# Late squares in one layer only, block weights with priority, and copies ahead of cuts in a two-layer decoder trunk

## The chip, the cores and the metric

The kernel runs on one core of a Trainium2 chip. The metric is device time in microseconds (us) of one execution. TensorE (PE in the profile) multiplies matrices and loads weights (PEld), VectorE (DVE) and ScalarE (ACT) work on tiles, GpSimd (POOL) does small odds and ends, SyncE (SP) starts the DMAs.

## The reference

Two layers work on 512 tokens of width 1024, in float32. Layer 0 mixes by sliding-window attention and a short gated convolution, layer 1 by chunked gated linear attention. Behind its mixer each layer has a gated MLP with a convolution over tokens and then a gate on a per-layer embedding:

```python
x = x + _conv_ffn(_rms_norm(x, ffn_norm[i]), ffn_w_up[i], ffn_conv_w[i], ffn_conv_b[i], ffn_w_down[i])
x = x + _per_layer_embedding(x, p[i], ple_norm[i], ple_w_gate[i], ple_w_proj[i])

def _per_layer_embedding(x, p_i, norm, w_gate, w_proj):
    gate = jax.nn.sigmoid(_rms_norm(x, norm) @ w_gate)
    return gate * (p_i @ w_proj)
```

The RMS norm needs, for each token, the sum of squares over the 1024 features. The kernel multiplies by the unnormed operand and scales the result by the norm afterwards, so the sums are needed later than the operand.

## The kernel before

**Data.** The stream `x` is kept as eight tiles `xT[m]` of 128 features by 512 tokens. A float32 product is made of three matmuls: each operand is split into a rounded high part (ACT copies it, `wh` for weights) and the rest (DVE subtracts, `wl`). `cut` and `cut_blocks` do this for weights, `split` for activations. Weights arrive by DMA in a `raw` buffer, two of which take turns; `wh` and `wl` have three buffers each.

**Seven products.** Where a block product allows it, `seven` computes a 2 x 2 block product with seven block multiplications in place of eight. It needs sums and differences of blocks on both sides. For weights these are made by `first_forms` (L864, L865) and `more_forms` (L872, L875) on DVE and cut at L840 (ACT) and L841 (DVE): `plain`, `t13`, the narrow `t2`, and `last`. For activations they are made by `blocks`: row m is scaled by the norm's gain (L302), and for each pair of rows the forms `e1`, `s12`, `o`, `s34` are built (L316 to L322 on DVE) and split (L109 on ACT, L110 on DVE). `seven` is a generator. Between its products ACT copies partial results from one PSUM bank to another (L897), because several results share a part; the product that follows in that bank waits for the copy.

**Squares.** `squares(m)` squares row m on ACT (L289 for row 0, L293 for the others) and adds it to `acc` on DVE (L294). `by_token` then transposes `acc` on PE (L345), and the sums and the inverse root are made from it. In `blocks`, the squares of both rows of a pair are traced behind the pair's forms and tied by `behind` to the last split, on ACT and on DVE; their scratch tile comes from `spare()`. Without `spare()`, `squares` takes its scratch from a tag "sq" with two buffers, which the narrow cut `t2` uses as well.

**Stages.** In each layer `ffn` runs the up-projection in groups, then `down`, whose last steps call `finish`, that is `blocks`, for each row. Then layer 0 runs `ple0` and layer 1 runs `ple1`. `ple0` has four stages g = 0 to 3. Each runs one `seven` for two output tiles, with the projection of the embedding in between, and `close` applies the gate of the stage before: DVE at L1408 to L1411, a sigmoid on ACT (L1414), DVE at L1415 and L1416, and then the squares for layer 1's first norm. `prepare` makes the weights of the next stage. In stage 0 the sums of squares are transposed between the third and the fourth step of `seven`. In stage 3 `enter` splits the rows for layer 1. `ple1` runs its products in an order written out by hand: the first product, two steps of the second, the transposes of `acc` at L345, and then the rest.

**Order.** Inside `manual_schedule(engines={ET.PE})` PE follows the written order; in `ple1`, ACT and DVE do as well. All other order on ACT and DVE is made by a planner when the program is built: of the instructions that are ready by its own costs, it takes the one traced first. `high_priority(offset=n)` moves instructions n places forward in that order. `issue_after(ins)` queues what is traced in it, on the engine of `ins`, behind `ins`, without a wait for its end. On the chip each engine takes its instructions in the planned order.

Of the kernel before, what the change touches and what calls it, by code (L numbers as in the profile page):

```python
# [63 lines left out]
class Kernel:  # L64
# [231 lines left out]
    def blocks(self, m, gain, scratch, tags, spare):  # L296


        nc = self.nc
        H = S // 2  # L300
        gx = scratch()
        nc.scalar.activation(gx, self.xT[m], AF.Copy, scale=gain[:, m : m + 1])  # L302

        def parts(x):
            w = x.shape[1]
            h, l = self.pair(self.fp, *tags)
            self.last_split = self.split((h[:, :w], l[:, :w]), x)
            return [(h[:, c], l[:, c]) for c in HALVES]

        if m % 2 == 0:  # L310
            self.even = gx
            self.e1 = parts(gx[:, :H])
        else:
            e, o = self.even, gx
            s12, s34 = scratch(), scratch()
            nc.vector.tensor_tensor(s12[:, :H], e[:, H:], o[:, H:], ALU.add)  # L316
            nc.vector.tensor_tensor(s12[:, H:], s12[:, :H], e[:, :H], ALU.subtract)
            s12p = parts(s12)
            op = parts(o)
            self.odd_split = self.last_split  # L320
            nc.vector.tensor_tensor(s34[:, :H], e[:, :H], e[:, H:], ALU.subtract)
            nc.vector.tensor_tensor(s34[:, H:], o[:, :H], s12[:, H:], ALU.subtract)  # L322
            s34p = parts(s34)
            self.forms.append(
                dict(e1=self.e1[0], o1=op[0], o2=op[1], s1=s12p[0], s2=s12p[1], s3=s34p[0], s4=s34p[1])
            )
            with self.behind(self.last_split):
                self.squares(m - 1, spare())
                self.squares(m, spare())

    @contextmanager
    def behind(self, pair):
# [552 lines left out]
    def seven(self, od, ws, x, keep=None, swift=False, pair=None):  # L885


        nc = self.nc
        H = S // 2
        mm = nc.tensor.matmul  # L890
        W, V = self.pa(), self.pa()[:, :H]
        X, Y = self.ps(), self.ps()
        plain, t13, t2 = ws

        def copy(out, src):
            with self.tc.high_priority(offset=60) if swift else nullcontext():
                return nc.scalar.copy(out, src)  # L897

        def product(out, w, c, x, first=False):
            kw = dict(skip_group_check=True)  # L900
            for j in range(ND // 2):
                (wh, wl), (xh, xl) = w(j, c), x(j)
                mm(out, wh, xh, start=first and j == 0, stop=False, **kw)  # L903
                mm(out, wh, xl, start=False, stop=False, **kw)  # L904
                mm(out, wl, xh, start=False, stop=j == ND // 2 - 1, **kw)  # L905

        left, right = HALVES
        product(W[:, left], plain, 0, x["e1"], True)
        copy(X[:, left], W[:, left])
        copy(Y[:, left], W[:, left])  # L910
        yield
        product(V, t13, 0, x["s1"], True)
        more = V
        if keep is not None:
            more = keep()
            copy(more, V)
        product(X[:, left], plain, 1, x["o1"])
        product(Y[:, left], t2, 0, x["s2"])
        yield copy(X[:, right], Y[:, left])
        with self.behind(pair):  # L920
            last = self.cut_blocks(od)
        product(X[:, right], t13, 1, x["s3"])
        yield copy(Y[:, right], X[:, right])
        product(Y[:, left], last, 1, x["s4"])
        product(X[:, right], last, 0, x["o2"])
        yield X, Y, more

    def ffn(self, i, project, next_gain):


        nc, a, tc = self.nc, self.a, self.tc
# [4 lines left out]
        mine, other = (("a0", "a1"), ("b0", "b1"))[:: 1 - 2 * i]  # L936
        with tc.tile_pool(name=f"ffn{i}", bufs=1) as fp:
# [4 lines left out]
            def both():  # L942
                return fp.tile([P, 2, S], F32, tag="zt", name=self.nm("zt"), bufs=2)
# [132 lines left out]
            steps, w0c, w1c = ready  # L1076
            with tc.manual_schedule(engines={ET.PE}):
                late = begin(0, steps, w0c)
                close = lambda: None
                for d in range(groups):  # L1080
                    g, y = both(), both()
                    copied = next(steps)
# [6 lines left out]
                    copied = next(steps)  # L1089
# [6 lines left out]
                    if d + 1 < groups:  # L1096
                        steps, w0c, w1c = prepare(d + 1, copied)
# [29 lines left out]
            def spare():  # L1127
                return fp.tile([P, S], F32, tag="z", name=self.nm("sq"), bufs=3)

            finish = lambda m: self.blocks(m, next_gain, half, mine if m < 4 else other, spare)  # L1130
            work = [lambda f=f: split_blocks(f) for f in (14, 16, 18, 20)]
            for f in (8, 10, 12):
                split_pair(f)
# [231 lines left out]
    def ple0(self, fp, both, next_gain):  # L1365


        nc, a, tc = self.nc, self.a, self.tc
        H = S // 2
        forms = self.forms  # L1370
        wg = a["ple_w_gate"][0].rearrange("(k p) n -> p k n", p=P)
        operands = {q: (lambda j, q=q: forms[j][q]) for q in ("e1", "o1", "o2", "s1", "s2", "s3", "s4")}
        groups = ND // 2

        def load(g):
            raw = self.raw(ND, 2 * P)
            nc.sync.dma_start(raw, wg[:, :, 2 * P * g : 2 * P * (g + 1)])
            return raw

        def result():  # L1380
            return fp.tile([P, S], F32, tag="z", name=self.nm("so"), bufs=3)

        def prepare(raw, odd=None, last=None):
            ev, od = self.by_parity(raw)
            return self.seven(od, self.seven_forms(ev, od, raw, odd), operands, lambda: result()[:, :H], True, last)

        pT = self.pT
        steps = prepare(load(0), self.odd_split, self.last_split)
        wj = self.wj

        def proj(m):
            pj = self.pa()
            c = slice(m * P, (m + 1) * P)
            for k in range(2):
                self.mm3(pj, [w[:, k, c] for w in wj], pT[k], start=k == 0, stop=k == 1)
            return pj

        def enter(*ms):
            for m in ms:
                hl = self.pair(self.fp, "b0", "b1")  # L1400
                self.split(hl, self.xT[m], next_gain[:, m : m + 1])
                self.xg.append(hl)

        def close(g, sums, pjs):
            X, Y, more = sums
            gates = both()
            h2 = lambda x: x.rearrange("p (u t) -> p u t", u=2)
            nc.vector.tensor_tensor(gates[:, 0], X, R, ALU.mult)  # L1408
            s = gates[:, 1]
            nc.vector.tensor_tensor(h2(s), h2(Y), more.unsqueeze(1).to_broadcast([P, 2, H]), ALU.add)  # L1410
            nc.vector.tensor_tensor(s, s, R, ALU.mult)  # L1411
            for c in range(2):
                m, s = 2 * g + c, gates[:, c]
                nc.scalar.activation(s, s, AF.Sigmoid)  # L1414
                nc.vector.tensor_tensor(s, s, pjs[c], ALU.mult)  # L1415
                nc.vector.tensor_tensor(self.xT[m], self.xT[m], s, ALU.add)  # L1416
                self.squares(m)

        late = None
        with tc.manual_schedule(engines={ET.PE}):  # L1420
            pjs = [proj(0), proj(1)]
            for g in range(groups):
                ends = g + 1 == groups
                if not ends:
                    raw = load(g + 1)
                next(steps)
                if late:
                    close(*late)
                if ends:
                    enter(0, 1)  # L1430
                next(steps)
                if ends:
                    enter(2, 3)
                if g:
                    pjs = [proj(2 * g)]
                else:
                    self.end_norm()
                    self.begin_norm(None)
                next(steps)
                if g:  # L1440
                    pjs.append(proj(2 * g + 1))
                last = steps
                if not ends:
                    steps = prepare(raw)
                late = g, next(last), pjs
                if g == 0:
                    R = self.spread()
            enter(4, 5)
            close(*late)
            enter(6, 7)  # L1450
        self.end_norm()
# [651 lines left out]
```

## Time and profile before

| | us |
|---|---|
| median of 3 runs | 1204.91 (1203.3 to 1205.11) |
| the profiled execution | 1205.17 |
| its span, first to last instruction | 1203.3 |
| PE busy in the span | 1190.9 |
| DVE busy | 993.7 |
| ACT busy | 690.4 |

The span is what the profile's views divide; 1.87 us of the execution lie around it. A row of the order in time has the start, the duration, the engine, the line, the operation, the tiles (out<-in), the shape and the count of instructions merged; a bracket at its end has the idle time of the engine before it and what ended it. Durations overlap a little, since the engines are pipelined. `ple0` runs from about 521 to 577 us, `ple1` from 1139 us to the end.

### The profile page before, as it was taken

To read this page: it belongs to the slowest core of one execution; us is meant where nothing else is said; L and a number is where in the kernel's file an instruction comes from. 1 tells how busy PE (TensorE), PEld (TensorE's weight loads), DVE (VectorE), ACT (ScalarE), POOL (GpSimd) and SP (SyncE) were. 2 spreads that over 40 slices of the span, in tenths; PEclk is the share of its full clock that TensorE was granted. 3 is DMA by queue.
4 is the path that set the end of the run, shared out by engine and by line. 5 is a ranking of instruction groups with operands and counts; after the bars stand their busy time and mean duration, and the time that the engine had idled before them with its cause. 6 is when DMAs were issued, how large, how long until landed. Compare 5 with 4: busy or idle time off the path is not lost.

```text
span 1203.3 us, 20222 instructions
## 1 busy us (share of the span) xinstructions
PE 1190.9 (99%) x8218; PEld 1081.1 (90%) x8218; DVE 993.7 (83%) x1593; ACT 690.4 (57%) x1137; POOL 45.5 (4%) x64
## 2 busy tenths in 40 slices
PE   9999999999999999999999999999999999999988
PEld 8877789999999989889878988899999999888877
DVE  6787687898999986899779876778989999978575
ACT  7466565656565653756563654555556556646364
POOL 2610000000000000000100000000000000000000
PEclk9999999999999999999999999999999999999999
DMA  7232222333332442321322212223242423323501
GB/s 222 72 99 78 74 88 71 107 105 106 106 106 89 147 133 89 105 71 61 120 87 70 89 53 75 84 93 118 72 141 71 130 81 115 125 86 123 184 1 70
DMA packets 112928, 117.76 MB, mean 98 GB/s; under 512 B 2840, under 2 KB 107858, under 8 KB 112836
## 3 DMA queue, kind: packets, MB, share of 16 engines
q1 hardware_dynamic: 112000, 115.88, 29.8%
q8 instruction: 64, 1.05, 0.4%
q0 software_dynamic: 560, 0.42, 0.3%
q14 instruction: 28, 0.23, 0.1%
q10 hardware_dynamic: 276, 0.18, 0.1%
HBM read 114.37 MB, written 2.10 MB: 97 GB/s over the span
## 4 chain that ended last, share of the span: by engine, by line
PE 89%; DVE 6%; ACT 3%; DMA 1%; issue 1%; POOL 0%; ACTq 0%; DVEq 0%
PE ps L171 11%; PE ps L172 11%; PE ps L173 11%; PE pa L173 7%; PE pa L172 7%; PE pa L171 7%; PE ps L903 6%; PE ps L905 6%; PE ps L904 6%; PE pa L905 2%; PE pa L903 2%; PE pa L904 2%; PE ps L1499 1%; PE ps L1501 1%; PE ps L1500 1%; DVE wl L152 1%
## 5 line engine op out<-in xcount | busy, mean ns | idle before, releaser
L152 DVE TENSOR_TENSOR wl<-raw,wh 128x1024 fp32r<-128x1024 f32 (+4 forms) x142 | 162.5, 1146 | 41.1 <-ACT wh L151 40.5
L151 ACT ACTIVATE wh<-raw 128x1024 fp32r<-128x1024 f32 (+4 forms) x142 | 141.2, 997 | 86.9 <-PE ps L172 54.4
L840 ACT ACTIVATE wh<-raw 128x1024 fp32r<-128x1024 f32 x90 | 95.4, 1062 | 128.3 <-DVE raw L865 86.2
L958 DVE SCALAR_TENSOR_TENSOR zt<-z,vfa,zt 128x510 f32<-128x510 f32 (+1 forms) x176 | 130.7, 743 | 0.3
L841 DVE TENSOR_TENSOR wl<-raw,wh 128x1024 fp32r<-128x1024 f32 x90 | 109.9, 1221 | 14.8 <-ACT wh L840 14.6
L173 PE MATMUL pa<-b,wl 128*128 128x256 f32 x352 | 97.3, 276 | 0.0
L173 PE MATMUL pa<-a,wl 128*128 128x256 f32 x352 | 97.3, 276 | 0.0
L172 PE MATMUL pa<-a,wh 128*128 128x256 f32 x352 | 97.2, 276 | 0.0
L171 PE MATMUL pa<-a,wh 128*128 128x256 f32 x352 | 97.2, 276 | 0.0
L171 PE MATMUL pa<-b,wh 128*128 128x256 f32 x352 | 97.2, 276 | 0.0
L172 PE MATMUL pa<-b,wh 128*128 128x256 f32 x352 | 97.2, 276 | 0.0
L956 ACT ACTIVATE zt<-z,vfb 128x512 f32<-128x512 f32 x88 | 71.3, 810 | 17.9 <-DVE z L948 8.8
L171 PE MATMUL ps<-b,wh 128*128 128x512 f32 x192 | 76.7, 399 | 0.1
L172 PE MATMUL ps<-b,wh 128*128 128x512 f32 x192 | 75.1, 391 | 0.0
L173 PE MATMUL ps<-b,wl 128*128 128x512 f32 x192 | 75.0, 391 | 0.0
L173 PEld LDWEIGHTS pa<-b,wl 128*128 128x128 f32 x352 | 66.1, 188 | 0.1
L172 PEld LDWEIGHTS pa<-a,wh 128*128 128x128 f32 x352 | 66.1, 188 | 0.0
L172 PEld LDWEIGHTS pa<-b,wh 128*128 128x128 f32 x352 | 66.1, 188 | 0.0
L171 PEld LDWEIGHTS pa<-a,wh 128*128 128x128 f32 x352 | 66.1, 188 | 0.0
L171 PEld LDWEIGHTS pa<-b,wh 128*128 128x128 f32 x352 | 66.1, 188 | 0.0
L173 PEld LDWEIGHTS pa<-a,wl 128*128 128x128 f32 x352 | 66.1, 188 | 0.0
L903 PE MATMUL ps<-four,wh 128*128 128x256 f32 x232 | 64.7, 279 | 0.0
(468 smaller groups left out, 3761.5 us busy)
## 6 DMA issues: line engine op xcount, KB each, us to landing
raw<-in_ffn_w_up_dram SPq DMA_DIRECT2D x42, 1024.0 KB, 5.0
raw<-in_ffn_w_down_dram SPq DMA_DIRECT2D x13, 1024.0 KB, 5.2
raw<-in_hy_w_in_dram SPq DMA_DIRECT2D x8, 1024.0 KB, 5.1
raw<-in_gla_w_in_dram SPq DMA_DIRECT2D x8, 1024.0 KB, 5.1
raw<-in_ffn_w_down_dram SPq DMA_DIRECT2D x8, 768.0 KB, 5.3
raw<-in_ple_w_gate_dram SPq DMA_DIRECT2D x6, 1024.0 KB, 5.5
raw<-in_hy_w_out_dram SPq DMA_DIRECT2D x16, 256.0 KB, 4.1
raw<-in_gla_w_out_dram SPq DMA_DIRECT2D x4, 1024.0 KB, 5.1
```

What stands on the lines that cost most here:

```text
L151: nc.scalar.activation(hv, v, AF.Copy)
L152: self.rest_cut = nc.vector.tensor_tensor(lv, v, hv.bitcast(F32), ALU.subtract)
L171: mm(out, lh, rh, start=start, stop=False, **kw)
L172: mm(out, lh, rl, start=False, stop=False, **kw)
L173: mm(out, ll, rh, start=False, stop=stop, **kw)
L840: nc.scalar.activation(h, src, AF.Copy)
L841: nc.vector.tensor_tensor(l, src, h.bitcast(F32), ALU.subtract)
L903: mm(out, wh, xh, start=first and j == 0, stop=False, **kw)
L904: mm(out, wh, xl, start=False, stop=False, **kw)
L905: mm(out, wl, xh, start=False, stop=j == ND // 2 - 1, **kw)
L956: nc.scalar.activation(y, z, AF.Identity, scale=w2[:, f : f + 1], bias=bb[:, f : f + 1])
L958: nc.vector.scalar_tensor_tensor(out=y[:, tap:], in0=z[:, : S - tap], scalar=w[:, f : f + 1], in1=y[:, tap:], op0=ALU.mult, op1=ALU.add,)
```

## The change

Three things are changed.

1. `blocks` in layer 1 is given no `spare`. There each row's squares are traced right after the row's own forms, with scratch from the tag "sq", and are tied to nothing. In layer 0 the squares stay as they were.
2. In `seven`, if `swift` is set (only `ple0` sets it), the cut of the last block weights (`last`: one ACT copy and one DVE subtraction) is moved 60 places forward in the planner's order.
3. In stage 0 of `ple0`, the weights of stage 1 are prepared under `issue_after(copied.ins)`: their ACT cuts are queued behind the copy from Y to X that the second step of `seven` gives back.

```diff
             self.forms.append(
                 dict(e1=self.e1[0], o1=op[0], o2=op[1], s1=s12p[0], s2=s12p[1], s3=s34p[0], s4=s34p[1])
             )
-            with self.behind(self.last_split):
-                self.squares(m - 1, spare())
-                self.squares(m, spare())
+            if spare:
+                with self.behind(self.last_split):
+                    self.squares(m - 1, spare())
+                    self.squares(m, spare())
+        if not spare:
+            self.squares(m)
...
         yield copy(X[:, right], Y[:, left])
-        with self.behind(pair):
+        with self.behind(pair), self.tc.high_priority(offset=60) if swift else nullcontext():
             last = self.cut_blocks(od)
...
-            finish = lambda m: self.blocks(m, next_gain, half, mine if m < 4 else other, spare)
+            finish = lambda m: self.blocks(m, next_gain, half, mine if m < 4 else other, None if i else spare)
...
-                next(steps)
+                copied = next(steps)
                 if ends:
                     enter(2, 3)
...
                 if not ends:
-                    steps = prepare(raw)
+                    with nullcontext() if g else tc.issue_after(copied.ins):
+                        steps = prepare(raw)
```

## The prediction

> **What bounds the kernel now.** I read the page first, then the stretches of the span, then the order in time of the three busy engines where the matmul engine stands still.
>
> ```profile
> span 1203.3 us, 20222 instructions
> PE 1190.9 (99%) x8218; PEld 1081.1 (90%) x8218; DVE 993.7 (83%) x1593; ACT 690.4 (57%) x1137; POOL 45.5 (4%) x64
> ```
>
> TensorE (PE) is busy 1190.9 of 1203.3 us, and the change adds or removes no matmul. So it can move the time only through the 12.4 us in which PE is idle, and through the speed at which PE runs. The view of stretches shows where these are: columns are the length, then busy time (and instructions) of PE, weight loads, DVE, ACT and POOL, then the granted clock, the DMA share and GB/s.
>
> ```profile
> 524.00:540.00 16.00, 14.40 (x112) 13.06 (x111) 14.81 (x25) 10.59 (x21) 1.43 (x1) 1.00 0.21 67
> 540.00:570.00 30.00, 30.00 (x232) 28.05 (x230) 28.22 (x41) 20.78 (x37) 0.00 (x0) 1.00 0.20 61
> 570.00:600.00 30.00, 28.98 (x172) 26.64 (x173) 21.23 (x32) 17.21 (x31) 3.87 (x7) 1.00 0.36 115
> 1139.00:1155.00 16.00, 12.59 (x55) 10.47 (x54) 12.93 (x19) 10.58 (x19) 0.00 (x0) 0.89 0.01 1
> 1155.00:1197.00 42.00, 42.00 (x206) 35.20 (x206) 29.77 (x36) 24.31 (x40) 1.91 (x1) 1.00 0.10 38
> ```
>
> Three of the places lie where the diff works: the first stage of `ple0` (1.60 us idle between 524 and 540), its last stage (1.02 us after 570), and the start of `ple1` in layer 1 (3.41 us idle, with a mean clock of 0.89). Stages 1 and 2 of `ple0`, which fill 540 to 570, have no PE idle at all. The largest place in order of time, PE first (a row's last bracket is the idle time before it and what ended it):
>
> ```profile
> 1146.19 0.39 PE L1501 MATMUL ps<-wh,b 128*128 128x512 f32 x1
> 1149.99 0.76 PE L345 MATMUL pa<-cf,acc 128*128 128x128 f32 x4 [3.41 <-DVE acc L294]
> ...
> 1154.13 0.39 PE L1501 MATMUL ps<-wh,b 128*128 128x512 f32 x1
> 1154.36 0.39 PE L1499 MATMUL ps<-four,a 128*128 128x512 f32 x1
> ```
>
> Then DVE and ACT at the same place:
>
> ```profile
> 1144.05 1.22 DVE L1488 TENSOR_TENSOR raw<-four,raw 128x1024 f32<-128x1024 f32 x1
> 1146.73 1.21 DVE L1488 TENSOR_TENSOR raw<-four,raw 128x1024 f32<-128x1024 f32 x1
> 1148.46 1.47 DVE L294 TENSOR_TENSOR acc<-acc,sq 128x512 f32<-128x512 f32 x2
> ```
>
> ```profile
> 1142.26 0.40 ACT L109 ACTIVATE a<-zt 128x256 fp32r<-128x256 f32 x1
> 1144.16 1.15 ACT L109 ACTIVATE a<-zt 128x512 fp32r<-128x512 f32 x2 [1.50 <-DVE zt L317]
> 1146.84 0.63 ACT L109 ACTIVATE a<-zt 128x512 fp32r<-128x512 f32 x1 [1.52 <-DVE zt L322]
> 1147.37 1.13 ACT L293 ACTIVATE sq<-xT 128x512 f32<-128x512 f32 x2
> ```
>
> PE reaches the transposes of the summed squares (L345) at 1146.42, since its matmuls follow each other by 0.23 us, and waits for `acc`. The two squares stand last on ACT (1147.37), because they are held behind the last split; their sums stand last on DVE (1148.46), behind two subtractions L1488 that prepare later weights. ACT meanwhile stood idle twice for 1.5 us.
>
> **Part 1: the squares of layer 1.** For layer 1 the diff takes away the tie to the last split and gives each row's squares their place right after its own forms. Nothing is added: eight squares on ACT and seven additions on DVE, as before. What PE can win back here is the wait, 1149.99 - 1146.42 = 3.57 us, and the slow stretch behind it. From 1149.99 to 1154.36 PE does 4 + 8 transposes and 6 matmuls in 4.37 us. The same work elsewhere:
>
> ```profile
> 810.74 0.44 PE pa L345 x4
> ...
> 501.55 1.03 PE L1359 MATMUL pa<-cf,pin 128*128 128x128 f32 x8
> 502.34 0.48 PE L171 MATMUL ps<-uh,wh 128*128 128x512 f32 x1
> 502.65 0.40 PE L172 MATMUL ps<-ul,wh 128*128 128x512 f32 x1
> ```
>
> 0.44 + 0.79 + 0.31 + 5 x 0.23 = 2.69 us, so the slow clock costs 1.68 us and the place 5.25 us in all.
>
> When do the sums land? ACT now meets square 6 after the first scaling and square 7 at the latest in the idle time behind 1145.31; the addition for row 7 then goes ahead of a subtraction L1488, which comes later in the program. If square 7 takes the first gap (from 1142.66), the sums end near 1145; if it takes the second, pushed back by square 6, it ends near 1145.31 + 2 x 0.57 = 1146.4 and its addition, after the forms that stand ahead of it, near 1147.9 to 1148.5. I take the first: ACT is idle there and nothing with an earlier place can use the gap. But not all of the 5.25 us comes through, because DVE is next in line:
>
> ```profile
> 1139.14:1149.95 10.81, 7.44 (x33) 5.82 (x31) 10.69 (x16) 6.35 (x10) 0.00 (x0) 1.00 0.00 0
> 1149.95:1152.85 2.90, 2.86 (x14) 2.76 (x15) 0.00 (x0) 2.06 (x4) 0.00 (x0) 0.58 0.03 6
> 1152.85:1162.35 9.50, 9.50 (x46) 7.90 (x45) 9.39 (x10) 7.99 (x18) 1.91 (x1) 0.95 0.00 0
> ...
> 1161.13 1.22 DVE L1479 TENSOR_TENSOR wl<-four,wh 128x1024 fp32r<-128x1024 f32 x1
> ...
> 1163.67 0.39 PE L172 MATMUL pa<-wl,four 128*128 128x512 f32 x1
> ```
>
> DVE works through this stretch almost without a gap, except for the 2.90 us that it shares with PE's wait. Packed tight, the cut of the projection weights (L1479 of 1161.13) ends at 1162.35 - 2.90 = 1159.45. PE reads it at 1163.67 now, so PE can come at most 4.2 us earlier before it waits there. That is late next. The same cap holds if the sums come a little late, up to a wait of 1 us. Behind it PE is full to 1197 with DVE at 29.77 of 42, so what is won is kept. Part 1: 4.2 us; ends 1.4 (a wait of 2.1 us left, the clock loss unchanged) and 5.25.
>
> The six other rows lie between 1100 and 1120, where DVE is nearly full. Their squares come earlier by some operations of 0.6 us. What could suffer are the cuts of the down weights:
>
> ```profile
> 1112.90 1.22 DVE L152 TENSOR_TENSOR wl<-raw,wh 128x1024 fp32r<-128x1024 f32 x1
> ...
> 1120.55 0.85 ACT L151 ACTIVATE wh<-raw 128x768 fp32r<-128x768 f32 x1 [1.04 <-PE ps L172]
> ```
>
> A cut starts when PE frees one of three buffers, as the one at 1120.55 does, and PE then turns to the next cut; the one that is whole at 1114.12 is needed from there on, two cuts after its own start. The cover is 6.4 us, the cost nothing; with the cover gone a square would cost its 0.6 us each. The squares also go to the two-buffer tag "sq", which the narrow block weights `t` use; PE has read those for the last time before the first square is due:
>
> ```profile
> L903 PE MATMUL ps<-b,t x20: 276/276/276, 530.4 to 1094.3; 128*128 128x256 f32 x20
> ```
>
> So that costs nothing either.
>
> **Part 2: stage 0 of `ple0`.** The three ACT cuts of stage 1's weights are queued behind the copy from Y to X; their seven DVE operations follow through their inputs, and the loads are issued outside the tie, so no DMA queue is passed.
>
> ```profile
> 530.23 2.00 ACT L840 ACTIVATE wh<-raw 128x1024 fp32r<-128x1024 f32 x2
> 532.14 0.37 ACT L897 COPY ps<-ps 128x256 f32<-128x256 f32 x1
> ...
> 531.21 0.66 PE L345 MATMUL pa<-cf,acc 128*128 128x128 f32 x4
> 532.56 0.38 PE L903 MATMUL ps<-a,wh 128*128 128x256 f32 x1 [0.70 <-ACT ps L897]
> ...
> 534.74 0.39 PE L903 MATMUL ps<-a,wh 128*128 128x256 f32 x1 [0.50 <-ACT ps L897]
> ```
>
> Two cuts of 1.0 us run back to back; the second belongs to stage 1 and holds the copy back to 532.14, although PE has Y ready at 531.26. Without it the copy runs at about 531.3, PE's next product starts behind the transposes at 531.9: 0.6 us. The second wait, 0.50, stays: there ACT is already idle. The cut that is put off ends near 532.7; its rest was cut at 533.07 anyway, and PE asks for it at 537.93. Queued behind the copy it costs nothing.
>
> **Part 3: the priority of the last block weights.** Its two operations move ahead of the gating work of the stage before. In stages 1 and 2 no PE idle can be won. In stage 3:
>
> ```profile
> 573.14 1.22 DVE L841 TENSOR_TENSOR wl<-raw,wh 128x1024 fp32r<-128x1024 f32 x1
> 574.42 0.39 PE L905 MATMUL ps<-a,wl 128*128 128x256 f32 x1 [0.92 <-DVE wl L841]
> ```
>
> The wait of 0.92 us goes. But parts 2 and 3 together (1.5 us) meet the end of layer 0, where PE needs the next norm's sums:
>
> ```profile
> 562.90:575.95 13.05, 12.13 (x92) 10.96 (x91) 13.05 (x19) 9.55 (x18) 0.00 (x0) 1.00 0.04 4
> 575.95:585.77 9.82, 9.82 (x63) 9.54 (x61) 9.23 (x16) 6.01 (x10) 1.97 (x5) 1.00 0.39 127
> ...
> 585.83 0.66 PE L345 MATMUL pa<-cf,acc 128*128 128x128 f32 x4
> ```
>
> DVE has 0.59 us of idle time in 23 us ahead of these transposes, which start as the sums end. A new order on DVE doesn't shorten its work, so about 0.6 us passes this point, and the rest turns into a wait there. Parts 2 and 3: 0.6 us; ends -1.2 (one cut of 1.22 us put ahead of the gating chain and not regained) and 1.5.
>
> **The sum.** The profiled execution took 1205.17 us around its span of 1203.3; the median of the runs is 1204.91, 0.26 lower, which I leave inside the range. 1205.17 - 4.2 - 0.6 = 1200.4.
>
> [...] The rows show that a wait of 0.92 us leaves the clock at 1.00 and one of 3.41 us is followed by 0.58; what a wait of 2 us does, they don't show. [...]
>
> **The rivals.**
> *The sums come only half earlier.* The order of ACT and DVE is made by a planner with its own costs; if square 7 gets its place behind the forms, `acc` ends near 1148.5 and a wait of 2.1 us stays. For it: the planner left ACT's first gap empty before, though the odd row's own split could have used it. Against it: the squares need only the row itself, which is there from 1140.5. 1205.17 - 1.4 - 0.6 = 1203.2.
> *Layer 1 stays as it is.* If the squares still follow the last split in the planner's order, part 1 is nothing and 1204.6 remains. Against it: square 6 comes ahead of row 7's scaling in the program.
> *Slower.* The squares among the cuts of the down weights between 1096 and 1120: ACT is served in order, so a square that waits holds every cut behind it. Eight squares of 0.57 us are 4.5 us on ACT. It decides only when the cuts lose their whole lead of 6.4 us and about 5 us more, the gain; the time would then pass 1205. Against it: the rows show the lead, and no square waits in that stretch.
>
> **How the numbers follow.** Forecast 0.60; better than it, with DVE's cap and the end of layer 0 both softer than worked out, 0.05 (1205.17 - 5.25 - 1.5 = 1198.4); half earlier 0.17; layer 1 unchanged 0.11; slower 0.07. The range goes from 1198.4 to 1204.6; the forecast's own, from 1199.0 to 1201.8. 0.2% is 2.4 us, about what a measurement of this kernel can tell from no change. Faster by more takes in the forecast, the better case and half of the first rival: 0.74; within it 0.19; slower 0.07.
>
> **What would show it.** Right: the wait for L294 before L345 in `ple1` under 1 us and the clock near 1.0 behind it; a new small wait of PE for L1479 before the first projection; L897 right behind PE at 531; no wait for L841 near 574, but one for L294 near 585. Wrong: `acc` later than 1147.5 on the old scale, or a PE wait for L151 or L152 in layer 1's down-projection.

## The result and the profile after

The changed kernel takes 1199.81 us (median of 7 runs, 1199.51 to 1201.23), beside 1204.91 us (1203.3 to 1205.77) for the kernel before. The ratio is 0.9962 with a 95% interval of 0.995 to 0.9973. A second set of runs on another occasion gave 1199.48 beside 1204.32 and the same ratio, 0.9962 (0.9949 to 0.9976). The forecast was 1200.4 and "faster".

The page of the changed kernel, its span and the busy times of the engines:

```profile
span 1197.5 us, 20218 instructions
PE 1188.8 (99%) x8218; PEld 1079.3 (90%) x8218; DVE 993.4 (83%) x1593; ACT 690.6 (58%) x1137; POOL 45.2 (4%) x64
```

Idle time of PE fell from 12.4 to 8.7 us, and PE's busy time by 2.1 us with the same 8218 matmuls, most of it where the mean clock was 0.89 and is now 1.00, as the next view shows. The line numbers of the changed kernel are three or four higher than those of before (L897 is now L900, L903 is L906, L1479 is L1483); L294 kept its number.

The view of stretches (length; busy time of PE, weight loads, DVE, ACT, POOL; granted clock; DMA share; GB/s):

```profile
524.00:540.00 16.00, 14.77 (x119) 13.80 (x118) 15.07 (x26) 11.80 (x23) 1.43 (x1) 1.00 0.20 67
540.00:570.00 30.00, 30.00 (x231) 28.30 (x230) 28.17 (x41) 19.86 (x36) 0.00 (x0) 1.00 0.22 65
570.00:600.00 30.00, 29.72 (x175) 27.38 (x174) 21.58 (x32) 18.08 (x31) 3.59 (x7) 1.00 0.36 117
1137.00:1153.00 16.00, 16.00 (x78) 13.39 (x78) 15.95 (x24) 12.43 (x26) 0.98 (x1) 1.00 0.00 1
1153.00:1191.00 38.00, 37.39 (x184) 31.03 (x183) 27.22 (x32) 22.30 (x32) 0.93 (x1) 1.00 0.11 42
```

In the fourth row PE has no idle time and the clock is 1.00, where before it stood idle for 3.41 us at a mean clock of 0.89. The last row has 0.61 us of new idle time. The first row still has 1.23 us (1.60 before), the third 0.28 us (1.02 before).

The start of `ple1` in layer 1, in order of time, first PE, then ACT, then DVE:

```profile
1144.76 0.39 PE L1505 MATMUL ps<-wh,b 128*128 128x512 f32 x1
1144.98 0.60 PE L348 MATMUL pa<-cf,acc 128*128 128x128 f32 x4
...
1156.74 0.39 PE L171 MATMUL pa<-wh,four 128*128 128x512 f32 x1
1157.74 0.50 PE L172 MATMUL pa<-wl,four 128*128 128x512 f32 x1 [0.61 <-DVE wl L1483]
```

```profile
1140.22 0.61 ACT L293 ACTIVATE sq<-xT 128x512 f32<-128x512 f32 x1
...
1141.65 0.61 ACT L293 ACTIVATE sq<-xT 128x512 f32<-128x512 f32 x1
1143.32 1.67 ACT L109 ACTIVATE a<-zt 128x512 fp32r<-128x512 f32 x3 [1.05 <-DVE zt L317]
```

```profile
1141.59 0.69 DVE L294 TENSOR_TENSOR acc<-acc,sq 128x512 f32<-128x512 f32 x1
1143.21 0.68 DVE L294 TENSOR_TENSOR acc<-acc,sq 128x512 f32<-128x512 f32 x1
1145.95 1.22 DVE L1492 TENSOR_TENSOR raw<-four,raw 128x1024 f32<-128x1024 f32 x1
...
1156.47 1.22 DVE L1483 TENSOR_TENSOR wl<-four,wh 128x1024 fp32r<-128x1024 f32 x1
```

Each square now follows its row's scaling, the second just ahead of ACT's idle time. The second sum ends at 1143.89 (1145.3 on the scale of before, since PE comes to this place 1.43 us earlier), the transposes of the sums (L348) follow PE's matmuls without a wait, and the projection reaches its weights 0.6 us before DVE has cut them.

Stage 0 of `ple0` and the start of stage 1, PE and then ACT:

```profile
530.18 0.66 PE L348 MATMUL pa<-cf,acc 128*128 128x128 f32 x4
530.70 0.39 PE L906 MATMUL ps<-a,wh 128*128 128x256 f32 x1
...
532.85 0.39 PE L906 MATMUL ps<-a,wh 128*128 128x256 f32 x1 [0.50 <-ACT ps L900]
...
539.69 0.38 PE L906 MATMUL ps<-a,wh 128*128 128x256 f32 x1 [0.64 <-ACT ps L900]
```

```profile
529.19 1.06 ACT L843 ACTIVATE wh<-raw 128x1024 fp32r<-128x1024 f32 x1
530.29 0.36 ACT L900 COPY ps<-ps 128x256 f32<-128x256 f32 x1
530.56 1.07 ACT L843 ACTIVATE wh<-raw 128x1024 fp32r<-128x1024 f32 x1
...
536.92 1.28 ACT L1417 ACT_TABLE_LOAD   x1
538.22 0.64 ACT L1417 ACTIVATE zt<-zt 128x512 f32<-128x512 f32 x1
...
539.28 0.63 ACT L900 COPY ps<-pa 128x256 f32<-128x256 f32 x2
```

The same place on ACT in the kernel before:

```profile
539.62 0.63 ACT L897 COPY ps<-pa 128x256 f32<-128x256 f32 x2
540.28 1.28 ACT L1414 ACT_TABLE_LOAD   x1
```

The copy of stage 0 now lies between the two cuts, and its wait of 0.70 us is gone. But 7 us later the planner puts the table load of 1.28 us and a sigmoid of 0.64 us ahead of stage 1's first copies, where they stood behind them before, and PE waits 0.64 us there. The copy of stage 0 was won, and the copies of stage 1 were lost.

### The profile page after: what moved, and what is told of

Its sections match the earlier page's. It is cut to its first block, busy times and chain, and to the rows that moved or that the text cites. A ratio compares the mean times of both kernels' runs of the same rounds, so it can differ in the third digit from the quotient of the medians.

```text
span 1197.5 us, 20218 instructions
## 1 busy us (share of the span) xinstructions
PE 1188.8 (99%) x8218; PEld 1079.3 (90%) x8218; DVE 993.4 (83%) x1593; ACT 690.6 (58%) x1137; POOL 45.2 (4%) x64
## 3 DMA queue, kind: packets, MB, share of 16 engines
q8 instruction: 64, 1.05, 0.4%
## 4 chain that ended last, share of the span: by engine, by line
PE 89%; DVE 7%; ACT 2%; issue 1%; DMA 1%; ACTq 0%; POOL 0%; DVEq 0%
PE ps L171 12%; PE ps L172 12%; PE ps L173 12%; PE pa L173 7%; PE pa L172 7%; PE pa L171 7%; PE ps L906 6%; PE ps L908 6%; PE ps L907 5%; PE pa L908 2%; PE pa L906 2%; PE pa L907 2%; PE ps L1505 1%; PE ps L1504 1%; PE ps L1503 1%; DVE wl L152 1%
## 5 line engine op out<-in xcount | busy, mean ns | idle before, releaser
L152 DVE TENSOR_TENSOR wl<-raw,wh 128x1024 fp32r<-128x1024 f32 (+4 forms) x142 | 162.7, 1147 | 41.7 <-ACT wh L151 41.0
L151 ACT ACTIVATE wh<-raw 128x1024 fp32r<-128x1024 f32 (+4 forms) x142 | 141.2, 997 | 83.6 <-PE ps L172 54.0
L906 PE MATMUL ps<-four,wh 128*128 128x256 f32 x232 | 64.6, 279 | 0.0
```

What stands on the lines that cost most here:

```text
L151: nc.scalar.activation(hv, v, AF.Copy)
L152: self.rest_cut = nc.vector.tensor_tensor(lv, v, hv.bitcast(F32), ALU.subtract)
```

## The experiments

The table gives, for each profiled run, the time between marks on PE, as differences of the start times of rows: from the first product of `ple0`'s stage 0 (524.20 in the kernel before) to the norm transposes of layer 1 (585.83), from these to the first gate product of the mixer (603.11), and from that to the first matmul behind `ple1`'s first projections (1166.16). Then follow the median and the ratio to the kernel before with its interval. Runs of the kernel before gave medians of 1204.13 to 1204.32 in these comparisons. Only the first two columns together hold the same work: where the transposes stand among the mixer's first matmuls is the planner's choice. In the kernel before and in the runs without parts 2 and 3, 53 of these matmuls stand ahead of them, in the rows "after", "after, again", "parts 2 and 3" and "after + projection cut first" 54, and in the other six 51, at 0.17 us each.

| kernel | to norm transposes | to gate product | to `ple1` mark | median | ratio |
|---|---|---|---|---|---|
| before | 61.63 | 17.28 | 563.05 | 1204.91 | |
| after | 60.28 | 17.10 | 559.02 | 1199.81 | 0.9962 (0.9950 to 0.9973) |
| after, again | 60.38 | 16.82 | 558.98 | 1199.48 | 0.9962 (0.9949 to 0.9976) |
| part 1 alone | 60.45 | 17.21 | 559.61 | 1200.39 | 0.9966 (0.9952 to 0.9979) |
| part 2 alone | 59.69 | 16.99 | 564.32 | 1203.82 | 0.9993 (0.9985 to 1.0002) |
| part 3 alone | 59.95 | 18.76 | 563.54 | 1205.74 | 1.0012 (1.0003 to 1.0021) |
| parts 2 and 3 | 60.03 | 16.94 | 564.09 | 1203.42 | 0.9994 (0.9985 to 1.0002) |
| late squares, new buffer | 60.66 | 17.28 | 562.90 | 1203.93 | 1.0000 (0.9991 to 1.0009) |
| sums' transposes later | 60.61 | 17.13 | 562.37 | 1203.35 | 0.9991 (0.9982 to 1.0000) |
| part 3, gate cut later | 59.80 | 17.94 | 563.54 | 1204.03 | 0.9997 (0.9988 to 1.0006) |
| after + projection cut first | 60.32 | 16.96 | 558.10 | 1199.34 | 0.9953 (0.9940 to 0.9965) |
| after + gating tied | 60.00 | 19.00 | 558.87 | 1201.62 | 0.9977 (0.9967 to 0.9987) |
| both | 59.76 | 18.73 | 558.39 | 1200.60 | 0.9966 (0.9953 to 0.9978) |
| both, gate cut later | 60.09 | 17.90 | 558.06 | 1198.58 | 0.9954 (0.9941 to 0.9966) |

**Part 1 alone.** The kernel before with the new places of the squares in layer 1 and nothing else.

```
+            if spare:
                 with self.behind(self.last_split):
...
+        if not spare:
+            self.squares(m)
...
-  finish = lambda m: self.blocks(m, next_gain, half, ..., spare)
+  finish = lambda m: self.blocks(m, next_gain, half, ..., None if i else spare)
```

> Only the squares of layer 1 come early; ple0 stays as it was. Theory (the squares' place carries the gain, DVE's later cut caps it): 4.3 us faster than before, near 1200.6; in ple1 no wait of PE for L294, clock 1.0 behind it, and a wait of about 0.6 us for the cut of the projection weights (L1479 in before's lines, L1482 here). Rival (the gain of the whole change came from ple0 as much as from here): under 3 us.

Measured: 1200.39 us, ratio 0.9966. In its view of PE's waits the one for L294 is not among the rows; these two are:

```profile
PE ps L908 <- DVE wl L844: 0.9, 1, 0.9
PE pa L172 <- DVE wl L1482: 0.6, 1, 0.6
```

The second is the projection weights' cut, which becomes late, as forecast. The first is `ple0`'s last block cut, which part 3 would have moved. So part 1 brings about 4.1 us (0.0034 x 1204.2; by the interval 2.5 to 5.8 us), and nearly all that the whole change brings.

**The order or the buffer.** The squares of layer 1 stay tied to the last split, but go to the buffers that the change gives them.

```
             with self.behind(self.last_split):
-                self.squares(m - 1, spare())
-                self.squares(m, spare())
+                self.squares(m - 1, spare and spare())
+                self.squares(m, spare and spare())
```

> The kernel before, with layer 1's squares written to the two-buffer tag that the change gives them, but still tied to the pair's last split. Theory (the order of the squares carries the gain of part 1, not their buffer): the squares stay last on ACT and their sums last on DVE, PE waits 3 to 3.6 us for L294 and the clock falls behind it; time 1203.5 to 1205, ratio 0.999 to 1.001. Rival (the buffer that the squares gave back is what helps): the wait is under 1.5 us and the time is near 1200.5.

Measured: ratio 1.0000. PE's timeline of this run:

```profile
1148.42 1.11 PE L345 MATMUL pa<-cf,acc 128*128 128x128 f32 x4 [3.42 <-DVE acc L294]
```

The wait is the old one, so the order of the squares is what part 1 earns by, not the buffer.

**Part 2 alone.** Stage 1's weight cuts are tied to the copy, without the priority.

```
-                next(steps)
+                copied = next(steps)
...
-                    steps = prepare(raw)
+                    with nullcontext() if g else tc.issue_after(copied.ins):
+                        steps = prepare(raw)
```

> Only the cuts of ple0's stage 1 are queued behind the copy from Y to X. Theory: the copy starts at once when PE has Y ready, the 0.70 us wait in stage 0 goes and 0.6 us are won; the wait of 0.92 us in stage 3 stays. Since VectorE is full ahead of layer 1's norm, at most 0.6 us reaches the end: 1204.3. Rival (VectorE doesn't cap it there): the 0.8 us that the trace of the whole change shows between the transposes and the next product come through in full. Second rival: nothing measurable, 1204.9.

Measured: ratio 0.9993 (0.9985 to 1.0002). In its trace PE's way through `ple0` is short, 59.69 + 16.99 = 76.68 us against 77.66 to 77.94 in the three runs that have neither part 2 nor part 3 and no late cut (part 1 alone, late squares, later transposes). The expectation that the wait of 0.92 us in stage 3 stays was wrong: it is gone without the priority, since DVE has the last block cut ahead of the sums here,

```profile
569.59 1.22 DVE L841 TENSOR_TENSOR wl<-raw,wh 128x1024 fp32r<-128x1024 f32 x1
570.73 0.69 DVE L294 TENSOR_TENSOR acc<-acc,sq 128x512 f32<-128x512 f32 x1
```

and behind them in the run with late squares, which has the old order:

```profile
571.11 0.68 DVE L294 TENSOR_TENSOR acc<-acc,sq 128x512 f32<-128x512 f32 x1
571.71 1.22 DVE L841 TENSOR_TENSOR wl<-raw,wh 128x1024 fp32r<-128x1024 f32 x1
```

The wait for L294 in `ple1` stays, and its slow stretch was twice as long as in the kernel before (6.82 us beside 3.41; 564.32 in the third column); the section on the hardware shows the rows.

**Part 3 alone.** Only the priority of the last block weights.

```
-        with self.behind(pair):
+        with self.behind(pair), self.tc.high_priority(offset=60) if swift else nullcontext():
             last = self.cut_blocks(od)
```

> Only the last block weights of ple0 get their priority. Theory: the wait of 0.92 us for them in stage 3 goes, but the gating work of stage 2 is pushed back by 1.22 us of VectorE time and PE waits for the sums at layer 1's norm instead; 0 to 0.6 us won, near 1204.6. Rival: PE's 0.9 us come through in full, near 1204.0. A loss of over 0.5 us would say that the new small wait for L900 in stage 1 (0.64 us in the whole change) is its work and isn't paid back.

Measured: ratio 1.0012 (1.0003 to 1.0021). The wait for L841 near 574 is gone, and the norm transposes come early (59.95), but the way from there to the gate product is 1.5 us longer, of which two matmuls that stood ahead of the transposes before make 0.33 us. The two columns together, 78.71 us, are 0.8 to 1.1 us longer than in the runs that have neither part. The expectation put a loss of this kind on the copies of stage 1; that stage took 12.81 us, as in the kernel before (12.82), so the loss lies elsewhere. The view of PE's waits has a row that the kernel before has not:

```profile
PE pa L1731 <- ACT glr L1667: 1.1, 1, 1.1
```

And ACT's timeline shows why:

```profile
591.06 0.63 ACT L1722 ACTIVATE wgs<-wgu 64x512 fp32r<-64x512 f32 x1 [8.24 <-DMA wgu<-in_gla_gate_bias_dram]
591.60 1.04 ACT L151 ACTIVATE wh<-raw 128x1024 fp32r<-128x1024 f32 x1
...
593.31 0.27 ACT L1667 ACTIVATE glr<-ps,rtok 128x16 f32<-128x16 f32 x1
```

In the kernel before the weight cut L151 comes first (589.82), and ACT waits for the gate weights' load behind it. Here the gate cut L1722 stands ahead of it, so the weight cut waits for that load too, and with it the copies of `glr` that PE needs. One more order has turned over, 7 us earlier on DVE. The last cut of the mixer's first weights and the load that SP's queue issues when it frees their buffer, in this run:

```profile
582.96 0.69 DVE L294 TENSOR_TENSOR acc<-acc,sq 128x512 f32<-128x512 f32 x1
...
584.22 0.92 DVE L152 TENSOR_TENSOR wl<-raw,wh 128x736 fp32r<-128x736 f32 x1
```

```profile
585.21 1.47 SPq L120 DMA_DIRECT2D raw<-in_gla_w_in_dram  x2
```

And in the changed kernel:

```profile
581.12 0.92 DVE L152 TENSOR_TENSOR wl<-raw,wh 128x736 fp32r<-128x736 f32 x1
...
583.22 0.68 DVE L294 TENSOR_TENSOR acc<-acc,sq 128x512 f32<-128x512 f32 x1
```

```profile
582.07 3.44 SPq L120 DMA_DIRECT2D raw<-in_gla_w_in_dram  x2
```

With part 3 alone this cut goes behind the sums of the norm. That brings the norm transposes forward, and puts the next weights' load 3.1 us back. No edit touches these lines: the planner's order turned over 10 to 15 us behind the edit, presumably because the work ahead of it got other times in the planner's own costs; that was not followed.

**Parts 2 and 3 without part 1.**

```
 (the two edits above together)
```

> Both edits of ple0, the squares of layer 1 as before. Theory of the prediction: VectorE's 0.59 us of idle time ahead of layer 1's norm is the cap, 0.6 us won, near 1204.3. Rival from the trace of the whole change: 1.3 to 1.5 us come through, near 1203.5, because the sums themselves end earlier. In ple1 the 3.4 us wait and the slow clock stay in both.

Measured: ratio 0.9994 (0.9985 to 1.0002), or 0.7 us with an interval from 1.8 us gained to 0.2 us lost. This is near the 0.6 us of the theory, and the 0.9993 of part 2 alone can't be told from it. Way through `ple0`: 60.03 + 16.94 = 76.97 us. The order in the mixer did not turn over.

**The gate cut behind the weight cut.** Part 3 alone, with the cut of the gate weights split off their loads (`gate_up` now issues the loads alone) and queued on ACT behind the first cut of the query weights.

```
-            wgs = gate_up()
+            cut_gate = gate_up()
...
             w = pair_w(0)
+            with tc.issue_after(self.first_cut.ins):
+                wgs = cut_gate()
```

> Part 3 alone, with the cut of layer 1's gate weights (wgs) queued on ACT behind the first cut of the first query weights; nothing else is moved on purpose. Part 3 alone measured 1.0012 of the time before. Theory (the loss comes from ACT standing still behind the gate weights' load while the copies of glr wait): the 8 us idle time of ACT ahead of wgs goes, the stretch from the norm transposes to the first gate product takes about 17.2 us instead of 18.8, and the ratio falls to about 0.999 to 1.000. Rival (the loss comes from another place): that stretch gets shorter, but the ratio stays at 1.001.

Measured: ratio 0.9997 (0.9988 to 1.0006), 1.7 us below part 3 alone by the medians; the two intervals overlap a little. The stretch fell from 18.76 to 17.94 us, not to 17.2. ACT is still idle for 8 us ahead of the weight cut:

```profile
590.60 1.06 ACT L151 ACTIVATE wh<-raw 128x1024 fp32r<-128x1024 f32 x1 [8.21 <-DMA raw<-in_gla_w_in_dram]
591.57 0.25 ACT L1669 ACTIVATE glr<-ps,rtok 128x16 f32<-128x16 f32 x1
```

So the ratio came out as expected, and the stretch got shorter by less: the gate cut no longer holds ACT, the copies of `glr` begin 1.74 us earlier, and what is left of the wait is the load of the query weights itself, which is issued as late as in part 3 alone (584.78). On the same work, the first two columns together, 78.71 us fell to 77.74, which is the value of the runs that have neither part (77.66 to 77.94). So the order of the gate cut accounts for the loss. What keeps part 3 from gaining anything is then probably the late cut on DVE, to judge by ACT's wait for the load that follows it; a run that moves that cut alone was not made.

**The sums' transposes six matmuls later.** The kernel before, with PE doing twelve instead of six matmuls of the last group ahead of the transposes of the sums. This measures a wait of about half the length.

```
-            add(None, "s1", wt1, first=True, order=steps[:2])
+            add(None, "s1", wt1, first=True, order=steps[:4])
...
-            add(None, "s1", wt1, order=steps[2:])
+            add(None, "s1", wt1, order=steps[4:])
```

> The kernel before, with the transposes of the sums put two steps (six matmuls, 1.36 us) later in the written order of ple1. PE's wait for L294 should shrink from 3.41 to about 2.05 us, at the same work. It asks what a wait of 2 us does to the clock. If the slow stretch behind the wait grows in proportion to it, or stays whole, 1.4 us are won: 1203.5. [...]

Measured: 1203.35 us, ratio 0.9991 (0.9982 to 1.0000). The wait fell to 2.06 us, and the clock still fell to 0.50, from 1150.90 to 1154.31. The slow stretch stayed whole (3.41 us, as in the kernel before), one of the two cases for which 1203.5 was expected. The third column gained 0.5 us on the run with late squares and 0.7 us on the kernel before, not the 1.35 us that the wait lost; 0.6 us of the rest went near 868 us, in layer 1's up-projection, where two of PE's products start right behind the DVE cuts of their weights. No edit touches that place, and other runs lose time there too, part 1 alone among them.

**Taking the new wait away.** The changed kernel, with the projection weights cut ahead of the last group's weights.

```
-            wt3 = chunks(b12)
             wj = chunk(wj_raw[:, 2:, :])
+            wt3 = chunks(b12)
```

> The changed kernel, with the cut of the projection weights written ahead of the two cuts for the product after it, on ACT and DVE. Theory (DVE's work caps part 1 at this cut): the wait of 0.61 us for it goes, PE is at the next product by 0.6 to 1.0 us earlier, and what is won reaches the end: 1199.0 to 1199.3. Rival: the wait only moves to the cuts that are now second (each 1.2 us of DVE), and the time stays at 1199.8.

Measured: 1199.34 us, ratio 0.9953 (0.9940 to 0.9965). The second matmul of the projections, which reads these weights, has no wait ahead of it:

```profile
1156.74 0.39 PE L172 MATMUL pa<-wl,four 128*128 128x512 f32 x1
```

The third column fell by 0.9 us, from 559.0 to 558.1. By the ratios alone this version can't be told from the change itself.

**The copies of stage 1 first.** The changed kernel, with the gating work of stage 0 queued on ACT and elsewhere behind stage 1's first two copies, so that the table load doesn't go ahead of them.

```
-                next(steps)
+                turned = next(steps)
                 if late:
-                    close(*late)
+                    with tc.issue_after(turned.ins):
+                        close(*late)
```

> The changed kernel, with the gating work of ple0 queued on ACT behind the stage's first two copies. Theory (the 0.8 us won by the copy in stage 0 are lost again in stage 1, because the planner put the table load and a sigmoid, 1.8 us of ACT, ahead of the first copies): the wait of 0.64 us for L900 near 539.7 goes, stage 1 is 0.6 to 1.0 us shorter. What reaches the end is bounded by the sums at layer 1's norm: 0.3 to 0.9 us, 1199.0 to 1199.5. Rival: the gate comes later, the sums with it, and PE waits for L294 near 584 instead; no gain or up to 0.5 us lost.

Measured: 1201.62 us, ratio 0.9977 (0.9967 to 0.9987), 1.8 us above the changed kernel by the medians. The wait for the copies near 539.7 went, but stage 1 took 14.16 us in place of 13.77, with new waits of 0.5 and 0.3 us for the narrow block cut, which now stands on ACT behind the table load and the sigmoid (540.06); and the planner's order in the mixer turned over as it did with part 3 alone, so the second column went from 17.1 to 19.0.

**Both together, both with the gate cut later, and the changed kernel once more.** The edits are those above; the three expectations stand in this order.

> The changed kernel with both edits, the cut of the projection weights first and the gating work behind the first copies. Theory: the two gains lie 550 us apart and add up, 0.9 to 1.9 us under the changed kernel: 1198.0 to 1199.0. Rival: neither passes on, 1199.8.

> The changed kernel, with the projection weights' cut first, the gating work of stage 0 queued behind the first two copies of stage 1, and the gate weights' cut queued as in the run beside it. The version without the last edit measured 0.9966. Theory: the stretch from the norm transposes to the first gate product goes from 19 to about 17.2 us, 1.5 us or a little more come back, and the ratio is about 0.9945 to 0.9955, 1198.3 to 1199.5 us, at or a little below the changed kernel beside it. Rival: the price paid in stage 1 of the gating (0.4 us) and what PE meets behind the gate product take it back; ratio 0.996.

> The changed kernel once more, beside the three others on the same chip. Expected: ratio 0.995 to 0.997. It tells how far the 0.9953 of the version with the projection weights' cut first and the version beside it can be told from the change itself, and whether PE's stages in the gating block come at the same times again (transposes for the sums near 530.2, spread near 535.7, norm transposes near 584.3).

Measured: 1200.60 (0.9966) with the order turned over, above both expected times, 1198.58 (0.9954) with the gate cut tied, 1199.48 (0.9962) for the changed kernel beside it, whose stages came at the expected times again (530.32, 535.91 and 584.48). The tie of the gate cut took 0.83 us from the second column here as well (18.73 to 17.90), and the medians fell by 2.0 us. The last version is 0.9 us below the changed kernel by the medians of five runs each, 1198.05 to 1198.90 against 1199.06 to 1200.28. The traces don't show that its edits earn this. The projection cut takes 0.9 us from the third column, but the way through `ple0` (60.09 + 17.90 = 77.99 us) is 0.6 to 0.8 us longer than the changed kernel's (77.20 and 77.38); the profiled execution is ahead by another 0.6 us at the first product of `ple0` (523.49 against 524.10), before any edit acts, where the fourteen traces differ by up to 0.9 us.

## Why the prediction was right

**The sum.** Forecast were 4.2 us for part 1 and 0.6 us for parts 2 and 3. Part 1 measured 4.1 us by its ratio, and 4.0 us in the traces of the kernel before and the changed kernel (563.05 to 559.02, third column). In its own trace it is 3.4 us (to 559.61), because that run lost 0.6 us near 868: PE's product starts at 868.19 behind a cut that DVE ends at 868.13, and in the changed kernel the same cut ends 0.3 us ahead of its product. Parts 2 and 3 measured 0.7 us by the ratio of the two alone, with an interval that takes in zero; by the traces 0.6 us, which is the mean way through `ple0` of the three runs that have neither and no late cut (77.94, 77.74, 77.66) less that of the three that have both (77.38, 77.20, 76.97).

**Part 1, the squares.** Right in each step. Square 7 took its place ahead of ACT's first idle time, the sums ended at 1143.9 (1145.3 on the old scale; forecast near 1145), the wait of 3.57 us and the slow stretch are gone, and the clock is 1.00. The run with late squares shows that this order is the cause. DVE's cap showed too: the forecast said that PE could come at most 4.2 us earlier before it waited for the projection weights, and it waits 0.61 us for L1483. Cutting these weights first gives 0.9 us more in the trace, which is about the 1.05 us that the forecast held back between the place (5.25) and the cap (4.2).

**The rival "slower"** had the earlier squares hold up the cuts of the down weights between 1096 and 1120. PE's waits in the changed kernel have no new row for L151 or L152. The rival "half earlier" did not occur. Its terms were tried by the later transposes: with a wait of 2.06 us the clock fell to 0.50 for 3.41 us, so the price of 1203.2, which kept the clock loss, was the right one in kind.

**Part 2.** The local step was right: the copy follows PE at 530.29, and the wait of 0.70 us is gone (530.18 to 530.70 in place of 531.21 to 532.56). The step that failed is the one on what comes after it, "queued behind the copy it costs nothing". The cut itself cost nothing, but the gating work that the planner places by its own clock moved ahead of stage 1's copies, stage 1 took 13.77 us in place of 12.82, and at the start of stage 2 the 0.7 us was gone again. The run with part 2 alone shows the same (13.77). That the order of these copies alone makes the loss is not shown: with the gating tied their wait was gone, and stage 1 took 14.16 us.

**Part 3.** The wait of 0.92 us for L841 went, and PE met a new one of 0.28 us for L1411 two us later. Stage 3 got 0.4 us shorter: from its first product to the norm transposes 22.26 us in both runs of the changed kernel, and 22.62 to 22.66 in the three runs without the parts. This mark has one of the mixer's matmuls more ahead of it in the changed kernel, so on the same work it is 0.5 to 0.6 us. But the wait is gone in the run with part 2 alone too, whose first two columns (76.68 us) are the shortest of all; no run shows that part 3 adds anything to part 2. What the forecast had not seen is that the priority can turn over the order of cuts on DVE and ACT 10 to 15 us later. Alone it made the kernel slower; with part 2 it does not happen.

**The cap at the end of layer 0** was about right in size, but its step "the rest turns into a wait there" failed. The forecast let 0.6 us through because DVE had 0.59 us of idle time ahead of the sums, and named a wait for L294 near 585 as its sign. There is no such wait: the sums of the changed kernel end at 583.90 and the transposes start at 584.29, when PE is ready for them; the planner had put one more matmul ahead of them. Measured from the first product of `ple0`, the sums end at 59.9 and 60.0 us in the two runs of the changed kernel, and at 60.3 to 60.5 us in the three runs without the parts, so they come 0.3 to 0.6 us earlier. Whether DVE sets that limit is open: with part 3 alone the sums end at 59.6 us, since the cut of 584.22 comes behind them, so DVE's work ahead of them can get shorter. The 0.6 us on the same work, the first two columns together, come from stage 3 onwards: from its first product to the gate product 39.1 and 39.4 us in the changed kernel against 39.8 to 39.9 us in the three runs without the parts. From stage 0 nothing is left; stage 3 starts 38.0 and 38.1 us behind the first product, against 37.8 to 38.0. That 0.6 us was forecast and 0.6 us measured is in part luck: the gain of stage 0 was lost again, the wait at the sums did not come, and part 2 alone won 1.1 us by its trace.

**The base.** The forecast started from a profiled execution of 1205.17 us. In that execution one down-weight cut came later than in any other profile:

```profile
502.69 0.85 ACT L151 ACTIVATE wh<-raw 128x768 fp32r<-128x768 f32 x1 [1.50 <-PE pa L1359]
```

The same cut in the changed kernel:

```profile
501.65 0.85 ACT L151 ACTIVATE wh<-raw 128x768 fp32r<-128x768 f32 x1 [0.65 <-DMA raw<-in_ffn_w_down_dram]
```

Measured from the first product of `ple0`, the cut lies 21.5 us ahead in the kernel before and 22.2 to 22.6 us ahead in the thirteen others, and the transposes of `ple0`'s sums come 7.01 us behind that product in place of 6.26, the value of two runs with the same order there. The way to the norm transposes, 61.63 us, is 1.0 us longer than in those two runs (60.66 and 60.61). So the two traces differ by 5.7 us, of which the change explains 4.6 to 4.8; how the late cut turns into the late transposes was not followed. The runs' medians of the kernel before are 0.3 to 1.0 us below 1205.17, and the forecast of 1200.4 came out 0.6 us above the measured 1199.81.

## What to carry to other kernels

Small work that only a later engine needs, and that is tied behind everything else, can sit at the very end of a chain; look at what the tie lets stand idle before it (here twice 1.5 us on ACT) and give it that place. Then ask which operation is late next, from the packed work of the engine behind it: that cap was worth 1 us here, and its sign showed as forecast.

Where a planner sets the order, a priority or a tie at one place is never local: compare the order of each engine's instructions for the next 20 us, look for an operation that needs a load moving ahead of one that does not, and test each part of a change alone, because a part can lose time alone (part 3), or do by itself what another part was made for (part 2).

## What the runs showed of the hardware

In the seven kernels that wait 2.06 to 3.42 us for the sums in `ple1`, the granted clock falls to 0.50 behind the start of this wait. The view of the slow stretch, cut at the points where the granted clock changes, for the run with the later transposes (wait 2.06 us):

```profile
1150.90:1154.31 3.41, 3.41 (x12) 2.73 (x10) 1.86 (x2) 3.41 (x7) 0.00 (x0) 0.50 0.02 5
```

And for part 2 alone (wait 3.42 us), in two rows:

```profile
1146.84:1150.25 3.41, 2.53 (x13) 2.53 (x13) 0.72 (x2) 1.38 (x3) 0.00 (x0) 0.50 0.02 5
1150.25:1153.66 3.41, 3.41 (x10) 2.73 (x9) 2.73 (x3) 3.41 (x12) 0.00 (x0) 0.50 0.00 0
```

And for the run with late squares (wait 3.42 us):

```profile
1148.02:1151.43 3.41, 3.01 (x13) 2.95 (x14) 0.34 (x1) 1.86 (x3) 0.00 (x0) 0.50 0.02 5
```

In these profiles the slow stretch lasts 3.41 us in the kernel before, with late squares, with later transposes and in the two kernels with part 3 alone, and 6.82 us in part 2 alone and in parts 2 and 3. It begins 2.1 us (parts 2 and 3) to 3.8 us (the kernel before) after PE stopped, in the first of these before PE starts again and in the second behind that. So one and the same wait of 3.42 us was followed by 3.41 us at half clock with late squares and by 6.82 us with part 2 alone: from the sums' transposes to the `ple1` mark 15.96 and 17.34 us, the same work. What decides between the two was not shown.

The run with the gating tied has a wait of 1.35 us for `glr`. In the stretch that holds 1.21 us of it the clock is 1.00:

```profile
592.54:595.95 3.41, 2.03 (x9) 1.54 (x10) 2.33 (x3) 3.36 (x11) 0.00 (x0) 1.00 0.11 38
```

This is a second reason for the gain of part 1: behind the waits of 2.06 to 3.42 us the slow clock cost another 1.5 to 3.0 us, by an estimate from these rows (half of the time that PE was busy at half clock: 3.01 us with late squares, 2.53 + 3.41 us with part 2 alone), while the clock was 1.00 at the waits of 1.35 us (the row above), 0.92 us (the kernel before, 573.00 to 578.50) and 0.61 us (the changed kernel, 1157.00 to 1162.00).
